# A hybrid encoder of four layers: in the latent layer, the keys' transposes stand behind the queries' projection and transposes

## The chip, the cores and the metric

The kernel runs on one core of one Trainium2 chip. The metric is device time in microseconds (us), the median of several runs; less is better. The core has a tensor engine (PE, which multiplies matrices and also transposes them, always into the accumulation memory, PSUM), a vector engine (DVE), a scalar engine (ACT), a general engine (POOL, which cannot reach PSUM here and works in the other on-chip memory, SBUF), and a queue (SP) from which nearly all transfers are issued. Each engine works through its own queue in order and waits at semaphores for the others.

## The reference

The kernel computes four residual layers, x <- x + Mixer(RMSNorm(x)), over 512 tokens of width 1024, all in 32-bit floats. Layers 0 and 3 are gated short convolutions, layer 1 is an attention over 128 keys chosen by an indexer, layer 2 is the latent attention, which the change touches:

```python
def mla_mixer(xn, positions, w_in, q_lat_norm, kv_lat_norm, w_uq, w_ukv, q_norm, k_norm, w_out):
    cq, ckv, kr, z = jnp.split(xn @ w_in, cuts, axis=-1)            # 384, 256, 32, 1024 columns
    q = (rmsnorm(cq, q_lat_norm) @ w_uq).reshape(bsz, seq, C_HEADS, C_QK)        # 16 heads of 96
    kv = (rmsnorm(ckv, kv_lat_norm) @ w_ukv).reshape(bsz, seq, C_HEADS, C_NOPE + C_V)
    k_nope, v = kv[..., :C_NOPE], kv[..., C_NOPE:]                               # 64 and 64
    k = jnp.concatenate([k_nope, jnp.broadcast_to(kr[:, :, None, :], ...)], axis=-1)
    q = rmsnorm(q, q_norm)
    k = rmsnorm(k, k_norm)
    q = jnp.concatenate([q[..., :C_NOPE], rope(q[..., C_NOPE:], positions)], axis=-1)
    k = jnp.concatenate([k[..., :C_NOPE], rope(k[..., C_NOPE:], positions)], axis=-1)
    o = dense_chunk_attention(q, k, v, C_QK ** -0.5).reshape(bsz, seq, C_WIDTH)  # chunk-causal softmax
    return (o * jax.nn.silu(z)) @ w_out
```

## The kernel before

**Tiling.** The 512 tokens are four tiles of 128 (`NT = 4`). Weights come from memory in pieces (`raw`), and ACT and POOL split each into a coarse and a fine part (`whi`, line 161, and `wlo`, line 163), in an order that is fixed by `enter` and the same for the whole program. Each projection is three matmuls on these parts (lines 287 to 289).

**The latent layer.** The 16 heads are worked in four groups of four heads. `project(g)` makes what the attention needs of a group: `keys_values(g)` first, then `queries(g)`.

- `keys_values` projects keys and values (two weight tiles by four token tiles, 512 columns, bank "pt" or "pj"). ACT copies the keys' 64 columns of each head to `kk` and the values to `v` (lines 1043, 1044), POOL squares and DVE sums them. When all four token tiles are there, POOL takes the inverse root (`small_rsqrt`) and scales `kk` (line 1057) and writes the shared rotary part beside it (line 1058). Then `finish(h)` turns the four heads.
- `queries` projects the queries (three weight tiles by four token tiles, 384 columns), ACT copies, DVE and POOL rotate (`rotate`: line 568 on POOL, 572 on DVE, 575 on POOL; the result is `qk`). Then its own `finish(h)` turns the four heads.
- A head is turned by `to_features` (line 585): four transposes of 128 tokens each into one PSUM bank `p`, then one ACT copy of 96 x 512 (line 113) to `kT` or `qT`. The bank is "tr", of which there is one; outside of an attention (`early_turns`) every second turn takes the bank "o" instead, so that two alternate.

**The attention.** It goes pair of heads by pair of heads. The scores of a pair (line 1083, tile `s`) come in chunks of 128 + 256, 384 and 512 keys and take two banks, of which there is one set; DVE adds the mask and takes the minimum (line 655), ACT takes the exponential (line 658), POOL or ACT divides by the sum (lines 673, 675), PE turns the probabilities (line 685, tile `pt`), ACT or DVE copies them (lines 690, 688), and PE multiplies with the values (line 706, tile `o`). A `Filler` steps other work in between: `project(1)`, `project(2)`, a gate projection, `project(3)`, the other gate projections (`pz`). `project(0)` and two gate projections run ahead of the attention; behind it comes the output projection (`po`).

**What sets the order.** The program is written as above, and is built with `schedule_with_timeline_sim=True`: a scheduler orders the instructions of each engine anew from the written order and what depends on what. So a small change in the written order can move instructions of every engine in this layer.

Of the kernel before, what the change touches and what calls it, by code (L numbers as in the profile page):

```python
# [71 lines left out]
def encoder(ctx: ExitStack, tc: tile.TileContext, a, out, depth=4):  # L72
# [14 lines left out]
    def tile_of(tag, name, shape=(P, S), dtype=F32):  # L87
        return sb.tile(list(shape), dtype, name=name, tag=tag, bufs=BUFS[tag])
# [4 lines left out]
    def tiny(name, n, dtype=F32, tag="tiny"):  # L93
        return sb.tile([P, n], dtype, name=name, tag=tag, bufs=24)

    def bank(name, tag):
        return ps.tile([P, S], F32, name=name, tag=tag, bufs=BANKS[tag])
# [14 lines left out]
    def copy(o, x):  # L112
        act_e.activation(o, x, AF.Copy)
# [163 lines left out]
    def small_rsqrt(v, n, scale, out=None):  # L277

        m = tiny("mean", n)
        pool.tensor_scalar(m, v, scale, EPS, op0=OP.mult, op1=OP.add)  # L280
        y = tiny("y", n) if out is None else out
        pool.tensor_tensor(out=y, in0=m, in1=minus_half[:, :n], op=OP.pow)  # L282
        return y
# [52 lines left out]
    def tokens_short(group, act, finish, tags):  # L336

        w = [x for _, u in units(group) for x in u]
        for t in range(NT):
            b = bank("pt", tags[t % len(tags)])  # L340
            for k in range(group.nk):
                products(b[:, :group.n], [y[:, t * P:(t + 1) * P] for y in act[k]], w[k], k == 0, k == group.nk - 1)
            finish(t, b)
            yield

    def by_head(x):
        return x.rearrange("p (t h) -> p t h", h=4)
# [214 lines left out]
    def rotate(o, x, C, T, bank=None):  # L562


        A, B, half = x.shape[1], x.shape[2], x.shape[4]
        pa = tile_of("rp", "ropea", (P, A, B, 2 * half))
        xf = x.rearrange("p a b i j -> p a b (i j)")
        pool.tensor_tensor(out=pa, in0=xf, in1=C.rearrange("p a i j -> p a (i j)")[:, :, None]
                                .to_broadcast([P, A, B, 2 * half]), op=OP.mult)
        pb = tile_of("rp", "ropeb", (P, A, B, 2, half))  # L570
        for i in range(2):
            dve.tensor_tensor(pb[:, :, :, i], (x if bank is None else bank)[:, :, :, 1 - i],
                                    T[:, :, None, i].to_broadcast([P, A, B, half]), op=OP.mult)
        e = dve if bank is None else pool
        e.tensor_tensor(out=o.rearrange("p a b i j -> p a b (i j)"), in0=pa,
                        in1=pb.rearrange("p a b i j -> p a b (i j)"), op=OP.add)
# [3 lines left out]
    def to_features(dst, src, n):  # L580

        turns[0] += 1
        p = bank("tr", "o" if early_turns[0] and turns[0] % 2 else "tr")
        for t in range(NT):
            pe.transpose(p[:n, t * P:(t + 1) * P], src(t), ident)  # L585
        clock[0] += 0.45
        if isinstance(dst, list):
            act_e.activation(dst[0], p, AF.Copy)
            dve.tensor_tensor(dst[1], p, dst[0].bitcast(F32), op=OP.subtract)
        else:  # L590
            copy(dst[:n], p[:n])
# [329 lines left out]
    def layer_c(last):  # L921
# [82 lines left out]
        def free(g):  # L1004

            return ["pj"] if g else ["pj", "pj", "pt", "pt"]

        def queries(g, qs, dst):
            raw = [None] * NT
            sums = tiny("hs", 16)  # L1010

            def fin(t, b):
                x = raw[t] = tile_of("qk", "qk", (P, 384))
                q = tile_of("rp", "qk2", (P, 384))
                x, b = (y.rearrange("p (h d) -> p h d", d=96) for y in (x, b[:, :384]))
                act_e.activation(x[:, :, 64:], b[:, :, 64:], AF.Copy)
                act_e.activation(q.rearrange("p (h d) -> p h d", d=96), b, AF.Square)
                dve.tensor_tensor(x[:, :, :64], b[:, :, :64], gqk[:, None].to_broadcast([P, 4, 64]), op=OP.mult)
                x5, b5 = (y[:, :, 64:].rearrange("p (a h) (i j) -> p a h i j", a=1, i=2) for y in (x, b))
                rotate(x5, x5, *(tab[:, t:t + 1] for tab in tq), b5)  # L1020
                dve.tensor_reduce(sums[:, 4 * t:4 * t + 4], q.rearrange("p (h d) -> p h d", d=96),
                                        axis=AX.X, op=OP.add)

            yield from tokens_short(a["c_uq"][g], lat["q"], fin, free(g))
            v = tiny("hv", 16)
            pool.tensor_tensor(out=by_head(v), in0=by_head(sums), in1=fq2[:, :, None].to_broadcast([P, NT, 4]),
                               op=OP.mult)
            y = small_rsqrt(v, 16, 1.0 / 96)
            pool.tensor_tensor(out=qs, in0=by_head(y), in1=fqs[:, :, None].to_broadcast([P, NT, 4]), op=OP.mult)

            def finish(h):
                to_features(dst[h], lambda t: raw[t][:, h * 96:(h + 1) * 96], 96)
            for h in range(4):
                finish(h)

        def keys_values(g, dst, vals):
            sums = tiny("hs", 16)
            ks = [tile_of("gate", "kk", (P, 4, 96)) for _ in range(NT)]

            def fin(t, b):  # L1040
                b3 = b.rearrange("p (h d) -> p h d", d=P)
                x3 = ks[t][:, :, :64]
                act_e.activation(x3, b3[:, :, :64], AF.Copy, scale=fkv[:, t:t + 1])
                act_e.activation(vals[t // 2][:, t % 2], b3[:, :, 64:], AF.Copy, scale=fkv[:, t:t + 1])
                q = tile_of("rp", "qk2", (P, 4, 64))
                pool.tensor_tensor(out=q, in0=x3, in1=x3, op=OP.mult)
                dve.tensor_reduce(sums[:, 4 * t:4 * t + 4], q, axis=AX.X, op=OP.add)

            yield from tokens_short(a["c_ukv"][g], lat["kv"], fin, free(g))
            v = tiny("hv", 16)  # L1050
            pool.tensor_tensor(out=by_head(v), in0=by_head(sums), in1=krs[:, :, None].to_broadcast([P, NT, 4]),
                               op=OP.add)
            y = small_rsqrt(v, 16, 1.0 / 96)
            for t in range(NT):
                x = ks[t]
                yt = y[:, 4 * t:4 * t + 4, None]
                pool.tensor_tensor(out=x[:, :, :64], in0=x[:, :, :64], in1=yt.to_broadcast([P, 4, 64]), op=OP.mult)
                pool.tensor_tensor(out=x[:, :, 64:], in0=krr[:, t, None].to_broadcast([P, 4, 32]),
                                   in1=yt.to_broadcast([P, 4, 32]), op=OP.mult)

            def finish(h):
                to_features(dst[h], lambda t: ks[t][:, h], 96)
            for h in range(4):
                finish(h)

        def masks(t):
            return cmask[:, S - (t + 1) * P:]
# [3 lines left out]
        def project(g):  # L1071
            s = sets[g] = dict(q=[tile_of("T", "qT") for _ in range(4)], k=[tile_of("T", "kT") for _ in range(4)],
                               v=[tile_of("v", "v", (P, 2, 4, 64)) for _ in range(2)],
                               qs=sb.tile([P, NT, 4], F32, name="qs", tag="qs", bufs=2))
            yield from keys_values(g, s["k"], s["v"])
            yield from queries(g, s["qs"], s["q"])

        def job(pair, after, fill):
            g, i = divmod(pair, 2)

            def scores(outs, t):
                for e, o in enumerate(outs):
                    pe.matmul(o, sets[g]["q"][2 * i + e][:96, t * P:(t + 1) * P],  # L1083
                              sets[g]["k"][2 * i + e][:96, :(t + 1) * P], start=True, stop=True)
                clock[0] += (t + 1) * P / 300
            return dict(scores=scores, masks=masks, after=after, fill=fill,
                        v=lambda e, t: sets[g]["v"][t // 2][:, t % 2, 2 * i + e],
                        qs=lambda e, t: sets[g]["qs"][:, t, 2 * i + e:2 * i + e + 1],
                        dst=lambda: gate[pair])

        z = a["c_z"]
        run(project(0))
        run(gate_steps(z[2:4], R, gate))
        ends = [0, 8, 16, 25, 34, 42, 50, 58, 66]
# [122 lines left out]
```

## Time and profile before

| | before |
|---|---|
| median of 3 runs | 1058.24 us (1058.1 to 1058.6) |
| the profiled execution's own time | 1058.71 us |
| its span, first to last instruction | 1056.9 us |
| granted TensorE clock, mean | 0.998 |
| PE busy in 500 to 600 us | 100.00 of 100 us |
| PE busy in 625 to 650 us (clock 0.93) | 23.32 of 25 us |
| PE busy in 650 to 675 us | 23.11 of 25 us |
| PE busy in 725 to 750 us | 23.44 of 25 us |
| PE busy in 735 to 815 us | 80.00 of 80 us |

The latent layer's work on groups of heads lies between some 608 and 815 us. A line of the timeline gives the start, the length up to the last end, the engine, the source line, the operation with what it writes and reads, the count, and in brackets how long the engine sat idle ahead of it and who ended that. PE's matmuls are pipelined: the next starts before the record of the one ahead of it ends, so that the step between two starts is shorter than a record. A line of a list of waits reads: who waited for whom, us in total, times, the longest. In a line of the windows stand the stretch and its length, then for PE, its weight loads, DVE, ACT and POOL the busy time and the number of instructions, then PE's granted clock, the transfers' share and GB/s.

### The profile page before, as it was taken

The numbers are of one execution on the slowest core, as the hardware profiler recorded it, in microseconds if no ns is written. First come the engines' busy times: TensorE is split into PE (matmuls) and PEld (weight loads), VectorE is DVE, ScalarE is ACT, GpSimd is POOL, SyncE is SP. The second block draws the span as 40 slices with busy tenths as digits, with TensorE's granted clock in tenths as the row PEclk, the third lists the DMA queues.
The fourth block names the chain that finished last, engine by engine and source line by source line (L and its number), as shares of the span: only waits on it lengthen the run. The fifth ranks groups of instructions, "written<-read, shape, count | busy, mean of one in ns | idle before, by whom it ended". The sixth has DMA issues, their size and how long they took to land.

```text
span 1056.9 us, 16253 instructions
## 1 busy us (share of the span) xinstructions
PE 1044.1 (99%) x6040; PEld 878.9 (83%) x6040; DVE 523.6 (50%) x1074; ACT 511.5 (48%) x1091; POOL 678.3 (64%) x636
## 2 busy tenths in 40 slices
PE   9999999999999999999999999999999999999998
PEld 7888888898898999898888787687777888888886
DVE  6884334335598974443435344444442664443321
ACT  6243223434444467676644446876764533333231
POOL 1546555666378799685538689788743856555552
PEclk9999999999999999999999999999999999999999
DMA  7233333224222221111213220101211333333332
GB/s 238 93 100 100 99 99 92 83 70 120 81 71 80 72 89 41 61 56 46 71 50 105 82 83 23 41 24 60 61 55 46 100 100 101 99 100 100 100 100 79
DMA packets 27295, 86.44 MB, mean 82 GB/s; under 512 B 3408, under 2 KB 4432, under 8 KB 27216
## 3 DMA queue, kind: packets, MB, share of 16 engines
q1 hardware_dynamic: 26928, 85.10, 25.9%
q8 instruction: 47, 0.77, 0.3%
q10 hardware_dynamic: 288, 0.31, 0.1%
q14 instruction: 32, 0.26, 0.1%
HBM read 83.30 MB, written 2.10 MB: 81 GB/s over the span
## 4 chain that ended last, share of the span: by engine, by line
PE 94%; DVE 2%; ACT 1%; POOL 1%; DMA 1%; issue 1%; ACTq 0%; POOLq 0%
PE pa L287 11%; PE pa L288 11%; PE pa L289 11%; PE po L287 6%; PE po L289 6%; PE po L288 6%; PE o L706 4%; PE pt L685 4%; PE s L1083 3%; PE pz L289 2%; PE pz L288 2%; PE pz L287 2%; PE s L296 2%; PE tr L585 2%; PE pq L287 2%; PE pk L288 2%
## 5 line engine op out<-in xcount | busy, mean ns | idle before, releaser
L163 POOL TENSOR_TENSOR wlo<-raw,whi 128x512 fp32r<-128x512 f32 (+4 forms) x320 | 401.4, 1262 | 281.4 <-ACT whi L161 269.4
L161 ACT ACTIVATE whi<-raw 128x512 fp32r<-128x512 f32 (+4 forms) x329 | 196.9, 603 | 328.9 <-PE pa L288 158.4
L288 PE MATMUL pa<-xl,whi 128*128 128x512 f32 x512 | 199.3, 389 | 0.0
L287 PE MATMUL pa<-xh,whi 128*128 128x512 f32 x512 | 198.2, 389 | 0.6 <-ACT xh L370 0.6
L289 PE MATMUL pa<-xh,wlo 128*128 128x512 f32 x512 | 197.6, 389 | 0.0
L287 PEld LDWEIGHTS pa<-xh,whi 128*128 128x128 f32 x512 | 96.0, 188 | 20.6 <-ACT xh L370 0.8
L288 PEld LDWEIGHTS pa<-xl,whi 128*128 128x128 f32 x512 | 96.1, 188 | 20.5 <-DVE xl L373 0.5
L289 PEld LDWEIGHTS pa<-xh,wlo 128*128 128x128 f32 x512 | 96.1, 188 | 20.0
L673 POOL TENSOR_SCALAR p<-p,rc 128x128 f32<-128x128 f32 (+1 forms) x64 | 70.2, 1103 | 45.9 <-DVE rc L668 40.6
L658 ACT ACTIVATE p<-p,mn 128x128 f32<-128x128 f32 (+3 forms) x128 | 71.0, 558 | 17.5 <-DVE mn L655 17.3
L480 DVE TENSOR_TENSOR cg<-pa,R 128x512 f32<-128x512 f32 x16 | 11.0, 690 | 118.5 <-PE pa L289 116.2
L655 DVE CUSTOM_DVE_ANT_0 p<-s,cmask,qs 128x128 f32<-128x128 f32 (+2 forms) x80 | 37.7, 506 | 33.9 <-PE s L1083 20.0
L287 PE MATMUL pz<-xh,whi 128*128 128x512 f32 x128 | 51.4, 401 | 0.0
L289 PE MATMUL pz<-xh,wlo 128*128 128x512 f32 x128 | 50.9, 398 | 0.0
L288 PE MATMUL pz<-xl,whi 128*128 128x512 f32 x128 | 50.4, 394 | 0.0
L288 PE MATMUL po<-xl,whi 128*128 128x512 f32 x128 | 50.1, 391 | 0.0
L288 PE MATMUL po<-glo,whi 128*128 128x512 f32 x128 | 49.8, 389 | 0.0
L282 POOL TENSOR_TENSOR y<-mean,minus_half 128x16 f32<-128x16 f32 (+1 forms) x18 | 49.2, 2732 | 0.8
L287 PE MATMUL po<-xh,whi 128*128 128x512 f32 x128 | 49.5, 400 | 0.0
L287 PE MATMUL po<-ghi,whi 128*128 128x512 f32 x128 | 49.5, 389 | 0.0
L690 ACT ACTIVATE p<-pt 128x384 f32<-128x384 f32 (+1 forms) x80 | 38.6, 510 | 22.0 <-PE pt L685 21.6
L685 PE MATMUL pt<-ident,p 128*128 128x128 f32 x320 | 47.9, 277 | 0.2 <-ACT p L690 0.2
(247 smaller groups left out, 2418.8 us busy)
## 6 DMA issues: line engine op xcount, KB each, us to landing
raw<-in_a_in SPq DMA_DIRECT2D x63, 512.0 KB, 3.9
raw<-in_a_out SPq DMA_DIRECT2D x16, 512.0 KB, 3.9
raw<-in_b_z SPq DMA_DIRECT2D x8, 512.0 KB, 3.5
raw<-in_b_q SPq DMA_DIRECT2D x8, 512.0 KB, 3.4
raw<-in_b_k SPq DMA_DIRECT2D x8, 512.0 KB, 3.7
raw<-in_b_v SPq DMA_DIRECT2D x8, 512.0 KB, 3.6
raw<-in_c_z SPq DMA_DIRECT2D x8, 512.0 KB, 3.6
raw<-in_b_out SPq DMA_DIRECT2D x8, 384.0 KB, 3.3
```

Of the source, the lines that this page charges most:

```text
L161: act_e.activation(hi[:, :, c], raw[:, j:j + m, c], AF.Copy)
L163: e.tensor_tensor(out=lo, in0=raw[:, j:j + m, :n - few], in1=hi[:, :, :n - few].bitcast(F32), op=OP.subtract)
L282: pool.tensor_tensor(out=y, in0=m, in1=minus_half[:, :n], op=OP.pow)
L287: nc.tensor.matmul(o, l[0], r[0], start=first, stop=False)
L288: nc.tensor.matmul(o, l[0], r[1], start=False, stop=False)
L289: nc.tensor.matmul(o, l[1], r[0], start=False, stop=last)
L655: dve.tensor_tensor_reduce(out=p[:, w], in0=banks[e][:, w], in1=j["masks"](t), scale=j["qs"](e, t), scalar=-GONE, op0=OP.add, op1=OP.min, ...
L658: act_e.activation(p[:, w], p[:, w], AF.Exp, bias=mn[e][:, i:i + 1], scale=-1.0, accum_out=sm[:, e * n + i:e * n + i + 1])
L673: pool.tensor_scalar(p[:, w], p[:, w], rc[:, i:i + 1], None, op0=OP.mult)
L685: pe.transpose(b[:, i:i + P], p[:, i:i + P], ident)
L690: act_e.activation(p[:, :n], b[:, :n], AF.Copy)
L706: pe.matmul(o[64 * e:64 * e + 64, t * P:(t + 1) * P], j["v"](e, kb), x[e][:, i:i + P], start=first, stop=t == 0)
```

## The change

In `keys_values` the loop that turned the four heads' keys goes; the function hands back the piece that turns one head, and `project` calls it for the four heads once `queries` has finished, its own turns included.

```diff
@@ keys_values
-            def finish(h):
-                to_features(dst[h], lambda t: ks[t][:, h], 96)
-            for h in range(4):
-                finish(h)
+            return lambda h: to_features(dst[h], lambda t: ks[t][:, h], 96)
...
@@ project
-            yield from keys_values(g, s["k"], s["v"])
+            turn_keys = yield from keys_values(g, s["k"], s["v"])
             yield from queries(g, s["qs"], s["q"])
+            for h in range(4):
+                turn_keys(h)
```

No instruction is added or taken away; the source lines from 1061 on move (the scores are line 1082 in the changed kernel). The transfers on SP keep their order. What the scheduler makes of it is seen at three places.

On PE, group 0, behind the last of group 1's keys' and values' projections (`pt` with 512 columns; `kk` are group 0's keys, `qk` its queries, `s` the first pair's scores, the last row begins group 1's queries' projection):

```order
 L288 MATMUL pt<-wlo,lhi 128x512
 L289 MATMUL pt<-whi,llo 128x512
-L585 MATMUL tr<-ident,kk 96x128 x16
-L585 MATMUL tr<-ident,qk 96x128 x4
+L585 MATMUL tr<-ident,qk 96x128 x12
+L585 MATMUL tr<-ident,kk 96x128 x12
+L1082 MATMUL s<-kT,qT 128x128
+L585 MATMUL tr<-ident,kk 96x128 x4
+L1082 MATMUL s<-kT,qT 128x128
+L1082 MATMUL s<-kT,qT 128x256 x2
 L287 MATMUL pt<-whi,lhi 128x384
```

Before, 16 transposes of keys and one head of queries stand here, then 18 projections, then the other three heads and the scores. After, twelve transposes of queries, the sixteen of keys and the scores stand here, and all projections behind them; four transposes of queries have gone ahead, two each among matmuls of the gate and of the projection. On POOL nothing moves up to this point: it still scales group 0's keys (lines 1057, 1058) ahead of the last two rotations (line 575).

On PE, group 2, its last three query heads before (the four key heads stand well ahead of these rows, each among other matmuls):

```order
L585 MATMUL tr<-ident,qk 96x128 x4
L1083 MATMUL s<-kT,qT 128x128
L585 MATMUL tr<-ident,qk 96x128 x4
L1083 MATMUL s<-kT,qT 128x128
L1083 MATMUL s<-kT,qT 128x256 x2
L585 MATMUL tr<-ident,qk 96x128 x4
L1083 MATMUL s<-kT,qT 128x384 x2
```

and the same heads and the keys behind them after the change (`p` are probabilities of an earlier pair, `o` its product with the values):

```order
L685 MATMUL pt<-ident,p 128x128 x6
L585 MATMUL tr<-ident,qk 96x128 x12
L585 MATMUL tr<-ident,kk 96x128 x4
L685 MATMUL pt<-ident,p 128x128 x8
L585 MATMUL tr<-ident,kk 96x128 x4
L1082 MATMUL s<-kT,qT 128x128
L706 MATMUL o<-p,v 64x128 x15
L585 MATMUL tr<-ident,kk 96x128 x4
L1082 MATMUL s<-kT,qT 128x128
L1082 MATMUL s<-kT,qT 128x256 x2
```

Four heads (twelve transposes and four) now follow each other with nothing between, and two more behind eight transposes of probabilities and behind the value matmuls. Group 1 has a like sequence, with six transposes of probabilities between some of the query heads.

On PE, group 3, after the change (`po` is the output projection; before, the key heads stand singly among matmuls of a gate, and each query head has other matmuls on both sides):

```order
L585 MATMUL tr<-ident,qk 96x128 x4
L706 MATMUL o<-p,v 64x128 x19
L585 MATMUL tr<-ident,qk 96x128 x4
L706 MATMUL o<-p,v 64x128
L585 MATMUL tr<-ident,kk 96x128 x8
L1082 MATMUL s<-kT,qT 128x128
L585 MATMUL tr<-ident,kk 96x128 x4
L1082 MATMUL s<-kT,qT 128x128
L1082 MATMUL s<-kT,qT 128x256 x2
L585 MATMUL tr<-ident,kk 96x128 x4
L287 MATMUL po<-xh,whi 128x512
```

and ACT's queue at the same place (`xh` is a gate tile's coarse part, `whi` weights of the output projection):

```order
L113 ACTIVATE qT<-tr 96x512 x3
L745 ACTIVATE xh<-gate 128x512
L113 ACTIVATE kT<-tr 96x512 x3
L658 ACTIVATE p,sum<-p,mn 128x128
L113 ACTIVATE kT<-tr 96x512
L658 ACTIVATE p,sum<-p,mn 128x256
L658 ACTIVATE p,sum<-p,mn 128x128
L658 ACTIVATE p,sum<-p,mn 128x256
L161 ACTIVATE whi<-raw 128x384
```

The last query head and the four key heads now stand together on PE, with single scores between some of them, and their copies stand together on ACT, ahead of exponentials and of a conversion of weights.

## The prediction

> **What bounds the kernel now.** I read the page's busy shares and its chain of waits first, then TensorE's list of waits in the latent layer (600 to 830 us), then its timeline there.
>
> ```profile
> span 1056.9 us, 16253 instructions
> PE 1044.1 (99%) x6040; PEld 878.9 (83%) x6040; DVE 523.6 (50%) x1074; ACT 511.5 (48%) x1091; POOL 678.3 (64%) x636
> PE 94%; DVE 2%; ACT 1%; POOL 1%; DMA 1%; issue 1%; ACTq 0%; POOLq 0%
> ```
>
> TensorE (PE) is busy for 99% and holds 94% of the chain: the kernel is as long as PE's matmuls plus PE's waits, and the change leaves all 6,040 matmuls in place. The DMA queue's order does not change at all. So the time can move by two things only: **how long PE waits, and at which clock it runs**. Nothing that ACT, POOL or DVE saves counts unless PE waits for it. In the latent layer PE waits for this:
>
> ```profile
> PE tr L585 <- ACT kT L113: 1.6, 2, 1.0
> PE s L1083 <- DVE mn L655: 1.5, 2, 1.1
> PE tr L585 <- POOL kk L1058: 1.0, 2, 0.5
> PE tr L585 <- ACT qT L113: 0.5, 1, 0.5
> PE pt L685 <- ACT p L690: 0.2, 1, 0.2
> ```
>
> That is 4.8 us shown as idle. A matmul's record lasts about 0.16 us longer than its place in the pipe, so a wait costs a little more than its idle time; below I count from start to start. The whole prize for a perfect order is some 8 us, 0.8% (4.6 in group 0, 1.8 in group 1 and 1.9 in group 2, all worked out below).
>
> **Group 0, where the keys' turns stand now.** TensorE's timeline (start, duration, operation, count, idle before):
>
> ```profile
> 638.80 0.89 PE L585 MATMUL tr<-ident,kk 128*96 128x128 f32 x4
> 640.18 0.42 PE L585 MATMUL tr<-ident,kk 128*96 128x128 f32 x2 [0.50 <-POOL kk L1058]
> 641.11 0.42 PE L585 MATMUL tr<-ident,kk 128*96 128x128 f32 x2 [0.51 <-POOL kk L1058]
> 642.11 1.57 PE L585 MATMUL tr<-ident,kk 128*96 128x128 f32 x8 [0.57 <-ACT kT L113]
> 643.50 1.09 PE L585 MATMUL tr<-ident,qk 128*96 128x128 f32 x4
> ...
> 645.03 0.52 PE L289 MATMUL pt<-whi,llo 128*128 128x384 f32 x1
> 645.35 0.52 PE L287 MATMUL pt<-whi,lhi 128*128 128x384 f32 x1
> ...
> 647.90 0.33 PE L288 MATMUL pt<-wlo,lhi 128*128 128x384 f32 x1
> 648.08 0.33 PE L289 MATMUL pt<-whi,llo 128*128 128x384 f32 x1
> 648.25 1.04 PE L585 MATMUL tr<-ident,qk 128*96 128x128 f32 x8
> 649.12 0.39 PE L1083 MATMUL s<-kT,qT 96*128 96x128 f32 x2
> ...
> 650.01 1.25 PE L1083 MATMUL s<-kT,qT 96*128 96x128 f32 x6
> 651.40 0.41 PE L287 MATMUL pt<-whi,lhi 128*128 128x384 f32 x1
> ```
>
> From 638.80 to 651.40, 12.6 us, PE does 32 transposes (eight take 649.12 - 648.25 = 0.87, so 0.11 each, 3.5 in all), 18 projections of 384 columns (0.17 each at 647.90, 3.1) and eight score passes (1.4): 8.0 us of work. The other 4.6 us are waits and a slow clock: at 645.03 a projection takes 0.32 instead of 0.17. The windows give the clock (the column behind POOL):
>
> ```profile
> 639.20:642.50 3.30, 1.66 (x10) 0.91 (x10) 0.01 (x1) 1.51 (x3) 3.25 (x8) 1.00 0.19 71
> 642.60:645.90 3.30, 3.30 (x15) 2.96 (x14) 0.55 (x2) 3.01 (x7) 3.22 (x5) 0.50 0.22 60
> 675.90:681.70 5.80, 5.80 (x40) 4.71 (x39) 2.98 (x11) 5.50 (x15) 2.17 (x3) 1.00 0.00 1
> 727.90:731.30 3.40, 2.17 (x14) 1.75 (x14) 1.44 (x9) 2.06 (x8) 3.32 (x5) 1.00 0.00 0
> ```
>
> A stretch of 3.3 us with only ten transposes is followed by one at half clock. Its price: five projections 0.15 late each (0.75), and ten or so transposes at twice 0.11, partly while PE waits anyway (0.75), 1.5 us. So group 0 holds 3.1 us of waits and 1.5 us of clock.
>
> **The same place after the change.** The keys' 16 transposes go behind the queries' 16, and the 18 projections of the next group that stood between them come after all. Four query transposes move ahead among other matmuls (4 x 0.11), so PE arrives at the other twelve at 638.80 + 0.44 = 639.24. These need the third and fourth quarter of the rotated queries, which POOL makes in the second of these rows (the first ends the scaling of the first quarter of the keys):
>
> ```profile
> 637.87 0.40 POOL L1058 TENSOR_TENSOR kk<-krr,y 128x128 f32<-128x128 f32 x1
> ...
> 641.02 0.86 POOL L575 TENSOR_TENSOR qk<-ropea,ropeb 128x128 f32<-128x128 f32 x2
> ```
>
> POOL's order is unchanged up to well behind this row: it still scales the keys first. The queries are ready at 641.45 and 641.88; the keys, ready from 638.27 on, must now wait behind them on PE. So **the wait for POOL is not removed but grows**: 2.6 us, against 1.0 idle now. Then six heads follow with nothing else between. The price of a head's turn in such a row:
>
> ```profile
> L113 ACT ACTIVATE kT<-tr x16: 573/589/604, 641.5 to 754.1; 96x512 f32<-96x512 f32 x16
> 726.81 0.60 PE L585 MATMUL tr<-ident,qk 128*96 128x128 f32 x4
> ...
> 728.09 0.64 PE L585 MATMUL tr<-ident,qk 128*96 128x128 f32 x4 [0.46 <-ACT qT L113]
> 731.35 1.56 PE L1083 MATMUL s<-kT,qT 96*128 96x384 f32 x4 [1.09 <-DVE mn L655]
> ```
>
> Four transposes end 0.60 after their start, ACT's copy takes 0.59, and with the hand-overs the bank is free again 728.09 - 726.81 = **1.28 us** after the first start. PE works 0.44 of it: a head that stands straight behind another costs 0.85 us of waiting in the attention, where all turns share the one bank "tr". Ahead of the attention two banks alternate, 0.64 per head. Walking on from 641.93 (the last query quarter): heads 2 to 7 start at 642.9, 643.5, 644.2, 644.8, 645.5 and 646.1, and the scores behind them end near 647.7. That is 8.45 us for 28 transposes and the scores (4.45): 4.0 of waits, against 3.1. **Term 0: +0.9.**
>
> For groups 1 to 3 I walked the new queues in the same way: an instruction starts when its engine is free and what it waits for has ended, with the durations of the rows of before.
>
> **Group 1.** Now:
>
> ```profile
> 657.50 1.88 PE L1083 MATMUL s<-kT,qT 96*128 96x512 f32 x4
> ...
> 661.27 1.58 PE L1083 MATMUL s<-kT,qT 96*128 96x128 f32 x8
> ...
> 664.65 1.46 PE L1083 MATMUL s<-kT,qT 96*128 96x384 f32 x4
> 667.13 0.64 PE L585 MATMUL tr<-ident,kk 128*96 128x128 f32 x4 [1.02 <-ACT kT L113]
> ...
> 670.81 1.06 PE L685 MATMUL pt<-ident,p 128*128 128x128 f32 x8 [0.18 <-ACT p L690]
> 659.81 0.73 DVE L655 CUSTOM_DVE_ANT_0 p<-s,cmask,qs 128x512 f32<-128x512 f32 x1
> 660.46 0.75 DVE L655 CUSTOM_DVE_ANT_0 p<-s,cmask,qs 128x512 f32<-128x512 f32 x1
> ```
>
> Start to start, its waits are 0.24 + 1.18 + 0.34 = 1.8. After: the second pair's scores stand straight behind the first's 512-column ones, with three transposes between. Those take 1.72 + 0.33 = 2.05, and the two score banks are free only when DVE has reduced both (1.4 more behind the scores' end; 3.77 lies between the two rows now): 1.2 to 1.7 of waiting, I take 1.3. The 512-column scores of that pair wait 0.65 for DVE in the same way, the value matmuls 0.75 and 0.3 for the copies of the probabilities, the last query head 0.65 and the first key head behind it 0.85. Sum 4.5. **Term 1: +2.7.**
>
> **Group 2.** Now 0.46 and 1.09 idle (the rows at 728.09 and 731.35), 1.9 from start to start. After, twelve query and four key transposes follow each other: three heads straight behind another, 2.55, and 0.5 at both ends. **Term 2: +1.2.**
>
> **Group 3.** Now PE never idles there, by the windows (the first number behind the length is PE's busy time):
>
> ```profile
> 735.00:815.00 80.00, 80.00 (x499) 63.20 (x500) 31.79 (x91) 51.54 (x131) 44.38 (x44) 1.00 0.19 52
> ```
>
> After, two key heads follow a query head with one matmul between (0.5 and 1.0, since ACT's queue has a conversion of the gate between two copies), a third 0.3, the output projection behind the last waits 1.3 for weights that ACT converts only behind these copies, and the next scores 0.8 for DVE. **Term 3: +3.9.**
>
> **The clock, term 4.** After the change there are three stretches of over 5 us in which PE has transposes and waits alone: group 0 from 639.24 to the first score near 645.9, group 1 (five heads among transposes of probabilities) near 5.8, group 2 near 7.7. Now there is one, 638.80 to 644.24, and it brought one half-clock stretch. At one each, that is two more at 1.5: **+3.0**. The rows speak for two readings. The 675.90 row has 40 matmuls, some of them scores, and the full clock; the 727.90 row is busy for 64% with eight transposes and scores, and the clock stays. If idle time alone decides, groups 1 and 2 are busy enough by their transposes and the term is near 0; if transposes don't count, it is larger, since the slow clock lasts until a stretch has enough matmuls. I take one each. The Trainium skill (TensorE: Matmul & The Clock Gate, "Part 4: PE-mode transpose") states that a transpose doesn't count as busy for the gate; the pair of rows at 639.20 and 642.60 agrees, but does not settle it, as PE also idled there.
>
> **Sum.** 0.9 + 2.7 + 1.2 + 3.9 + 3.0 = 11.7 us. The profiled execution took 1058.7 us (span 1056.9 and 1.8 around it), 0.5 over the runs' median of 1058.24: 1058.2 + 11.7 = **1070**.
>
> **Rivals.**
> - No further half clock: PE idles, but never so much as in the 639.20 row. The 64% busy row speaks for it. 1058.2 + 8.7 = 1067.
> - The slow clock lasts: two stretches of 3.4 us in each of the three places, six against one, 5 x 1.5 = 7.5, so 1058.2 + 8.7 + 7.5 = 1074. For it: ten transposes in 3.3 us did not keep the clock. By the skill's rule named above this one is right.
> - The waits move, but other work fills them: ACT and DVE have fewer pieces between, the copies come sooner, and 0.85 shrinks to what a head costs now. Then the order does nothing: 1058 to 1060. Against it: 1.28 us has only 0.1 of hand-over that could shrink.
> - Faster: the wait for POOL is gone, if the rotated queries are ready when PE arrives and the keys are long scaled behind them. Then group 0 loses its clock loss and most waits, 4.6 - 1.0, and the rest stays: 1054.6. It decides at 639.24: POOL would have to finish L575 2.6 us earlier, which the row at 641.02 speaks against.
>
> **How the numbers follow.** A measurement of this kernel can tell 0.2%, 2.1 us, from no change. Chances: forecast 0.45 (1068.5 to 1072), no further half clock 0.2 (1064 to 1068.5), longer half clock 0.23 (1072 to 1077), no effect 0.07, faster 0.05. The walk's waits are good to some 2 us (term 1's bounds alone are 0.5 apart, term 3 has no row of its own), so the range runs from 1063 to 1077: it holds the first three cases without their tails. Slower by over 0.2%: 0.9, within 0.2%: 0.05, faster: 0.05.
>
> **What would show it.** In the changed kernel's profile: PE "tr" waiting for POOL's qk (L575) some 2 us near 640; waits of "tr" for ACT's kT and qT of about 0.85 each, eight to ten of them, where now there are three; idle time of PE between 735 and 815 where now there is none; PEclk under 1.00 at three places instead of one. Wrong would be: heads in a row without such waits (the 1.28 us is no chain), or PE waiting as long as now and the time within 1060.

## The result, and the profile after

| | before | after |
|---|---|---|
| median | 1058.17 us (1057.85 to 1058.60) | 1069.24 us (1068.36 to 1069.99) |
| ratio, with its 95% interval | | 1.0104 [1.0091, 1.0117] |
| the profiled execution's own time | 1058.71 us | 1068.36 us |
| its span | 1056.9 us | 1066.6 us |
| granted TensorE clock, mean | 0.998 | 0.998 |

The kernel is slower by 11.1 us in the medians and by 9.7 us in the two profiled executions. The forecast was 1070. The first lines of the changed kernel's page, and TensorE's list of waits between 600 and 840 us (who waited for whom, us in total, times, the longest):

```profile
span 1066.6 us, 16250 instructions
PE 1046.0 (98%) x6040; PEld 878.5 (82%) x6040; DVE 522.8 (49%) x1074; ACT 512.9 (48%) x1091; POOL 679.4 (64%) x636
```

```profile
PE tr L585 <- ACT qT L113: 4.2, 7, 0.7
PE tr L585 <- POOL qk L575: 2.5, 2, 2.0
PE s L1082 <- DVE mn L655: 1.5, 3, 0.7
PE tr L585 <- ACT kT L113: 1.4, 2, 1.0
PE o L706 <- DVE p L688: 1.4, 3, 0.7
PE po L287 <- ACT kT L113: 1.1, 1, 1.1
PE pt L287 <- DVE ropeb L572: 0.7, 1, 0.7
...
```

PE has the same 6,040 matmuls and is busy for 1.9 us longer; its idle time in the whole list is 13.0 us (one wait of 0.2 is left out above), where it was 4.8. The 8.2 us of idle time and the 1.9 us of busy time are one thing: 20 waits stand here where 8 stood, and by the prediction's 0.16 us that a record is longer than its place in the pipe, twelve waits more are 1.9 us that count as busy. The waits for the keys on POOL are gone, and in their place stand two for POOL's rotated queries (L575), the longer one, in group 0, twice as long as both together were (2.0 against 1.0). The largest group is a turn that waits until ACT has emptied the bank of the query head before it, seven times, up to 0.7; before, it stood there once, with 0.5.

**Where the time is lost.** For the next table each kernel's PE was held against one yardstick: the mean step from one matmul's start to the next, for each form, from the trace of before with its waits left out. What a stretch takes beyond the sum of these steps is lost, by waits or by the clock. Only differences between columns count, good to some 0.3 us; the stretches are cut by time, so in a kernel that is already late their rows lie a little further on. The last four columns are the first four experiments below, in which a single group's keys are turned late.

| us lost by PE in | before | after | group 0 alone | group 1 alone | group 2 alone | group 3 alone |
|---|---|---|---|---|---|---|
| 638 to 656 (turns of group 0) | 5.1 | 5.7 | 5.7 | 4.1 | 4.2 | 5.1 |
| 656 to 712 (group 1) | 3.3 | 6.2 | 2.4 | 7.3 | 3.4 | 3.3 |
| 712 to 745 (group 2) | 3.2 | 5.4 | 3.2 | 3.7 | 7.9 | 3.1 |
| 745 to 815 (group 3) | 1.8 | 6.0 | 1.7 | 1.9 | 7.0 | 6.1 |

The change loses 0.6, 2.9, 2.2 and 4.2 us more in the four stretches, 10 us together, against 9.7 in the span.

PE's timeline after the change at three places, group 0, group 2 and group 3 (start, duration, operation, count, idle time before):

```profile
641.21 0.84 PE L585 MATMUL tr<-ident,qk 128*96 128x128 f32 x4 [2.02 <-POOL qk L575]
642.62 1.94 PE L585 MATMUL tr<-ident,qk 128*96 128x128 f32 x8 [0.57 <-ACT qT L113]
644.39 2.42 PE L585 MATMUL tr<-ident,kk 128*96 128x128 f32 x12
...
652.40 0.41 PE L287 MATMUL pt<-whi,lhi 128*128 128x384 f32 x1 [0.68 <-DVE ropeb L572]
...
720.67 0.64 PE L585 MATMUL tr<-ident,qk 128*96 128x128 f32 x4 [0.68 <-ACT qT L113]
722.00 0.64 PE L585 MATMUL tr<-ident,qk 128*96 128x128 f32 x4 [0.68 <-ACT qT L113]
723.32 0.64 PE L585 MATMUL tr<-ident,kk 128*96 128x128 f32 x4 [0.68 <-ACT qT L113]
...
726.04 1.96 PE L706 MATMUL o<-p,v 128*64 128x128 f32 x30 [0.53 <-DVE p L688]
...
782.22 0.64 PE L585 MATMUL tr<-ident,kk 128*96 128x128 f32 x4 [0.32 <-ACT qT L113]
783.82 0.64 PE L585 MATMUL tr<-ident,kk 128*96 128x128 f32 x4 [0.97 <-ACT kT L113]
...
785.14 0.64 PE L585 MATMUL tr<-ident,kk 128*96 128x128 f32 x4 [0.46 <-ACT kT L113]
...
788.44 0.50 PE L287 MATMUL po<-xh,whi 128*128 128x512 f32 x1 [1.13 <-ACT kT L113]
```

**Group 0:** PE idles 2.02 us ahead of 641.21 for POOL's last rotations. Of the keys, which stand behind them now, POOL has scaled two of the four quarters when this wait begins, the third at 639.81 and the last at 640.74. **Group 2**, from 720.67 on: three heads straight behind another, each 1.33 and 1.32 us after the one ahead, each idle for 0.68. **Group 3**, from 782.22 on: key heads behind key heads, and the first output projection 1.13 late behind the last copy. The same kernel's windows (stretch and length, then busy time and number of instructions of PE, weight loads, DVE, ACT and POOL, PE's granted clock, the transfers' share, GB/s):

```profile
639.02:642.43 3.41, 1.01 (x5) 0.34 (x4) 0.26 (x1) 1.19 (x3) 3.33 (x8) 1.00 0.14 55
642.43:645.84 3.41, 3.22 (x15) 2.67 (x16) 0.59 (x2) 2.13 (x5) 3.33 (x5) 0.50 0.22 58
717.52:720.93 3.41, 2.52 (x19) 1.78 (x18) 0.90 (x2) 2.68 (x6) 2.55 (x3) 1.00 0.11 46
720.93:724.35 3.42, 2.05 (x18) 1.55 (x17) 0.00 (x0) 1.54 (x3) 0.00 (x0) 1.00 0.00 0
735.00:815.00 80.00, 76.47 (x463) 60.12 (x462) 34.45 (x101) 53.72 (x136) 51.28 (x57) 1.00 0.18 50
```

Between 735 and 815 PE idles 3.5 us, where it idled none. And in the latent layer the clock is halved once only, in group 0, as before; in group 2, where PE has transposes and waits alone for two whole windows, it stays full.

### The profile page after: what moved, and what is told of

It is laid out like the page before. It is cut to its first block, busy times and chain, and to the rows that moved or that the text cites. A ratio compares the mean times of both kernels' runs of the same rounds, so it can differ in the third digit from the quotient of the medians.

```text
span 1066.6 us, 16250 instructions
## 1 busy us (share of the span) xinstructions
PE 1046.0 (98%) x6040; PEld 878.5 (82%) x6040; DVE 522.8 (49%) x1074; ACT 512.9 (48%) x1091; POOL 679.4 (64%) x636
## 4 chain that ended last, share of the span: by engine, by line
PE 94%; DVE 2%; ACT 2%; POOL 1%; issue 1%; DMA 1%; ACTq 0%; DVEq 0%; POOLq 0%
PE pa L287 11%; PE pa L288 11%; PE pa L289 11%; PE po L287 6%; PE po L289 5%; PE po L288 5%; PE o L706 4%; PE s L1082 3%; PE pt L685 3%; PE pz L289 2%; PE pz L287 2%; PE pz L288 2%; PE tr L585 2%; PE s L296 2%; PE pq L287 2%; PE pk L288 1%
## 5 line engine op out<-in xcount | busy, mean ns | idle before, releaser
L673 POOL TENSOR_SCALAR p<-p,rc 128x128 f32<-128x128 f32 (+1 forms) x64 | 69.9, 1098 | 70.7 <-DVE rc L668 66.5
```

The costliest lines, as they stand in the source:

```text
L673: pool.tensor_scalar(p[:, w], p[:, w], rc[:, i:i + 1], None, op0=OP.mult)
```

## The experiments

Theory A, as the expectations call it: PE's waits follow from the whole order of each queue, which the scheduler makes anew, so the price of the change isn't a sum of prices of groups. Theory B: each group's late turns have a price of their own, and these add up. Ratios are against the kernel before, with 95% intervals.

### One group alone

In the first four kernels, `e1_g0` to `e4_g3`, one group's keys are turned late and the other three groups' where they were (G is 0, 1, 2, 3):

```diff
-            for h in range(4):
-                finish(h)
+            [finish(h) for h in range(4) if g not in (G,)]
+            return finish
...
-            yield from keys_values(g, s["k"], s["v"])
-            yield from queries(g, s["qs"], s["q"])
+            turn_keys = yield from keys_values(g, s["k"], s["v"])
+            yield from queries(g, s["qs"], s["q"]); [turn_keys(h) for h in range(4) if g in (G,)]
```

> The keys' turns stand behind the queries for group 0 alone. Theory A (the time comes from PE's waits, and these depend on the whole order that the scheduler makes anew): walking this kernel's queues gives waits of +0.9 us over before, all near 640 to 650 (PE waits about 2 us for POOL's last two query rotations, then for ACT's copies). Theory B (each group has its own price and the prices add up to the 11 us): term 0 of the prediction, +0.9, and with the clock as before. Both: 1058.5 to 1060.5 us; groups 1 to 3 keep the waits of before.

> Group 1 alone. Theory A: the walk gives +5.4 us, of which some 3 lie in group 1 (scores behind scores waiting for DVE 1.4, two heads straight behind others 0.96 and 0.6) and over 1 in later groups that were not touched (value matmuls near 724, scores near 795): 1062 to 1065 us. Theory B: +2.7, 1060 to 1062 us, groups 2 and 3 as before.

> Group 2 alone. Theory A: the walk gives +7.3 us: four heads straight behind another at 0.86 each near 718 to 722, the next projection 0.84 behind the last copy, and 3.5 in group 3 and its scores, which were not touched: 1064 to 1067 us. Theory B: +1.2 to +3, 1059 to 1061.5 us. If transposes don't count as work for the clock gate, PEclk falls to half behind 718 to 726 for at least 3.4 us (+1.5); if idle time decides, it stays at 1.00.

> Group 3 alone. Theory A: the walk gives +3.0 us, with the output projection 0.9 behind ACT and score matmuls 1.8 and 0.5 behind DVE near 788 to 794, and no heads that wait 0.86: 1060.5 to 1062.5 us. Theory B: +3.9 with three heads waiting near 780, 1061.5 to 1063 us.

| late turns in | median us | ratio | us by the ratio |
|---|---|---|---|
| group 0 | 1058.47 | 1.0005 [0.9996, 1.0015] | +0.5 |
| group 1 | 1062.59 | 1.0043 [1.0028, 1.0058] | +4.6 |
| group 2 | 1068.12 | 1.0095 [1.0078, 1.0112] | +10.1 |
| group 3 | 1061.76 | 1.0038 [1.0023, 1.0053] | +4.0 |
| all four (the change) | 1069.24 | 1.0104 [1.0091, 1.0117] | +11.0 |

Group 0 alone came to the lower end of what both theories said, group 1 into theory A's range, group 3 into both ranges, and group 2 to more than both said. The four add up to 19 us and the whole change costs 11: theory B falls. The table of lost time says where. Group 1's stretch adds up (7.3 - 3.3 = 4.0 for its own edit, and 2.4 - 3.3 = -0.9 for group 0's, against 2.9 with all). Group 3's doesn't: its own edit costs 4.3 there and group 2's edit costs 5.2 there, though it leaves group 3's keys where they were; with both, 4.2. Nor is it the same loss. In the change it is mostly the key heads and the output projection that wait, as shown above. With one edit alone, the largest waits are those of the scores for DVE's minimum, 1.59 us at 794.61 in `e4_g3` and 1.53 us at 799.70 in `e3_g2`, and the window of 3.41 us behind each runs at half clock (the first two rows of the windows below), which makes its matmuls take some 1.7 us longer than by the yardstick. The edit of one group moves the work of the next, and each order has waits and slow windows of its own. That group 2 alone came to 10.1 has a second part, in group 2 itself, which its timeline and windows show:

```profile
720.44 0.64 PE L585 MATMUL tr<-ident,qk 128*96 128x128 f32 x4 [0.68 <-ACT qT L113]
...
723.09 0.64 PE L585 MATMUL tr<-ident,kk 128*96 128x128 f32 x4 [0.68 <-ACT qT L113]
724.41 0.64 PE L585 MATMUL tr<-ident,kk 128*96 128x128 f32 x4 [0.68 <-ACT kT L113]
724.89 0.39 PE L1083 MATMUL s<-kT,qT 96*128 96x128 f32 x2
725.73 1.09 PE L585 MATMUL tr<-ident,kk 128*96 128x128 f32 x4 [0.46 <-ACT kT L113]
...
799.70 2.01 PE L1083 MATMUL s<-kT,qT 96*128 96x384 f32 x4 [1.53 <-DVE mn L655]
```

```profile
795.80:799.21 3.41, 3.41 (x12) 2.40 (x11) 2.16 (x7) 2.67 (x8) 1.52 (x3) 0.50 0.00 0
800.67:804.08 3.41, 3.41 (x14) 2.45 (x13) 1.81 (x6) 2.22 (x6) 1.50 (x2) 0.50 0.01 2
...
722.16:725.57 3.41, 1.75 (x13) 1.06 (x10) 0.00 (x0) 1.67 (x3) 0.00 (x0) 1.00 0.00 0
725.57:728.98 3.41, 3.25 (x12) 2.72 (x13) 0.00 (x0) 0.70 (x2) 0.00 (x0) 0.50 0.00 0
```

The first row is `e4_g3`'s, the others are `e3_g2`'s. Five heads stand in a row here, without the eight transposes of probabilities that the change has between them. From 722.16 to 725.57 eight transposes and two scores start, and the clock is halved behind them (four transposes take 1.09 at 725.73, not 0.64). That is the loss that the prediction feared in three places; it comes in the experiments, and not in the change.

### POOL's wait in group 0

`c1_dve_keys0` leaves the written order as it was and scales group 0's keys on DVE; `c5_rot_dve` is the change with the latent layer's last rotation (L575) on DVE, so that the rotated queries no longer stand behind the keys on POOL:

```diff
# c1_dve_keys0, against before (lines 1057 and 1058)
-                pool.tensor_tensor(
+                (dve if g in (0,) else pool).tensor_tensor(
# c5_rot_dve, the change and in rotate (line 574)
-        e = dve if bank is None else pool
+        e = dve if bank is None or half == 16 else pool
```

> The kernel before, with group 0's keys scaled on DVE instead of POOL (8 instructions). Theory A (group 0's loss before is its wait for POOL, 1.0 us idle, and the half clock that follows): the keys are ready about 2 us earlier, PE's wait for POOL near 640 goes, and with less idle time the clock stays at 1.00 there: -1.6 us of waits by the walk and up to -1.5 us of clock, 1055 to 1056.5 us. Theory B (a run of transposes alone brings the half clock, whether PE idles or not): PEclk still falls to 0.5 behind 639 to 644, 1056.5 to 1057 us.

> The change, with the sum at the end of the latent layer's rotations (line 575, queries and shared key) on DVE instead of POOL. Theory A: the 2.0 us that PE waits for POOL near 640 go, since the last two rotations no longer stand behind the key scaling; the heads still stand in rows, so waits of 0.7 to 0.9 for ACT's copies stay, near 720 for four heads: the walk gives +6.5 us over before, 1062.5 to 1065 us, with the clock at 1.00 near 642. Theory B (the time lies in the rows of heads alone, POOL does not matter): as the change, 1068 to 1070 us.

`c1_dve_keys0` took 1056.30 us, ratio 0.9980 [0.9971, 0.9989]; `c5_rot_dve` 1064.45 us, 1.0053 [1.0036, 1.0070], both as theory A said. Group 0 with the late keys and without POOL's wait (PE's timeline of `c5_rot_dve`, then one of its windows in group 2):

```profile
636.86 1.03 PE L585 MATMUL tr<-ident,qk 128*96 128x128 f32 x8
...
640.49 1.03 PE L585 MATMUL tr<-ident,kk 128*96 128x128 f32 x8
642.10 0.64 PE L585 MATMUL tr<-ident,kk 128*96 128x128 f32 x4 [0.57 <-ACT kT L113]
```

```profile
718.62:722.03 3.41, 1.89 (x13) 1.13 (x11) 0.00 (x0) 1.30 (x3) 0.00 (x0) 1.00 0.00 0
```

The 2.02 us have gone, and in this execution the half clock with them: the stretch loses 2.5 us against 5.7 after the change and 5.1 before. So the wait ahead of 641.21 hangs on POOL's order, as its row says, though the scheduler made another order of PE's queue too: projections stand between the queries' and the keys' turns now. The edit moves the rotations of all four groups. The other three stretches still lose 4.2, 5.7 and 3.6 us, where the change loses 6.2, 5.4 and 6.0 and before 3.3, 3.2 and 1.8, and the kernel stays slower than before: what the change costs lies mostly in the attention, not where its wait is longest. The profiled execution is the fastest of this kernel's (1061.19 us at clock 1.000; the others 1063.87 to 1065.13 at 0.998 to 0.999), so these losses are on the low side.

### The bank that all turns share

`e9_onebank` takes from the latent layer's turns ahead of the attention their second bank; `e5_banks` gives those in the attention a second one, "pj". Both are the change, with line 583:

```diff
-        p = bank("tr", "o" if early_turns[0] and turns[0] % 2 else "tr")
# e9_onebank
+        p = bank("tr", "o" if early_turns[0] and n != 96 and turns[0] % 2 else "tr")
# e5_banks
+        p = bank("tr", ("o" if early_turns[0] else "pj" if n == 96 else "tr") if turns[0] % 2 else "tr")
```

> The change, with the one bank tr for all turns of heads in the latent layer, group 0 too. Theory A: a head straight behind another costs 0.85 us of waiting with one bank and 0.2 with two, so group 0's six heads in a row wait 0.85 each near 642 to 648, at least +2.5 us over the change; the scheduler also makes the later order anew, the walk gives +7 us over the change in all: 1073 to 1079 us. Theory B (the bank is no bound, ACT's copies are): no change, 1068 to 1071 us.

> The change, with every second turn of a head in the attention in one of the two banks pj. Theory B (a price per head times the number of heads in rows): with two banks the price falls from 0.85 to 0.2, some nine heads gain 0.65 each: 1062 to 1064 us. Theory A (the whole order decides): the waits of the turns fall in the same way, but the scheduler makes another order, in which PE waits for POOL's and DVE's work on the probabilities instead (2 to 3 us at single places near 710 and 757): 1068 to 1074 us.

`e9_onebank` took 1079.35 us (1078.16 to 1080.49), 1.0196 [1.0179, 1.0213], 0.35 us above theory A's range. Its group 0 (timeline, then a window):

```profile
643.01 1.09 PE L585 MATMUL tr<-ident,qk 128*96 128x128 f32 x4 [0.68 <-ACT qT L113]
644.78 1.09 PE L585 MATMUL tr<-ident,qk 128*96 128x128 f32 x4 [0.68 <-ACT qT L113]
```

```profile
641.20:658.20 17.00, 12.72 (x44) 9.09 (x45) 3.05 (x12) 6.95 (x16) 8.50 (x11) 0.50 0.04 12
```

With one bank the heads of group 0 queue up as those of the attention do, here 1.77 us apart since the clock is half, and it stays half for 17 us: heads in a row with their waits are too little work to bring it back. This stretch loses 12.6 us instead of 5.7.

`e5_banks` was to take 1062 to 1064 us by theory B and 1068 to 1074 by theory A. It took 1076.05 us (1073.42 to 1078.44), 1.0168 [1.0148, 1.0187]: theory B had the sign wrong, and theory A had the waits that would come, but too short. Its waits in the latent layer:

```profile
PE pt L685 <- POOL p L673: 8.6, 4, 3.8
PE s L1083 <- DVE mn L655: 4.6, 5, 1.3
...
PE tr L585 <- ACT qT L113: 0.9, 2, 0.6
...
PE tr L585 <- ACT kT L113: 0.5, 2, 0.2
```

The turns' waits for ACT fell from 5.6 us to 1.4, so it is the bank that they waited for. But the scheduler made another order of it, in which the transposes of the probabilities come up to 3.8 us too early for POOL's division (L673), 8.6 us in four waits, where the change has none. The clock is at half for 17 us more than in the change, too (from 666.99, 718.19 and 765.97 on, behind waits for DVE or POOL), which by the yardstick costs some 7 us. So this kernel shows what the turns waited for, and not what the change would cost with two banks in its own order.

### The order as written, and a spread

`f1_written_before` and `f2_written_all` are before and the change with the instructions in the written order, without the scheduler. `e6_spread` is the change with a step of the `Filler` behind each turned head, so that other work can stand between two heads:

```diff
# f1_written_before, f2_written_all
-    schedule_with_timeline_sim=True
+    schedule_with_timeline_sim=False
# e6_spread, against the change, in queries
             for h in range(4):
-                finish(h)
+                to_features(dst[h], lambda t: raw[t][:, h * 96:(h + 1) * 96], 96)
+                yield
# and in project
-            for h in range(4):
-                turn_keys(h)
+            yield from (turn_keys(h) for h in range(4))
```

> The kernel before, built without the scheduler, each engine in the written order. Much slower than before, since nothing fills PE's waits: 1130 to 1170 us by a walk of the queues. It is the base for the next run.

> The change, built without the scheduler. Theory A (the 11 us come from the order that the scheduler makes of the change, not from the later turns of the keys themselves): in the written order the change moves little or gains, since the keys' scaling on POOL has the queries' projection as cover: 0 to 4 us below the run before this one. Theory B (turning the keys behind the queries is itself what costs): about 10 us above it.

> The change, with the fill of the attention allowed to go on to other work between any two of the eight turns (a yield behind each head). Theory A: the scheduler makes nearly the same queues from it, the walk gives +9.7 us over before, and heads still wait 0.85 in rows: 1067 to 1070 us. Theory B (the four turns stand in rows because project hands them out in one piece): the heads spread among other matmuls and the time falls to 1058 to 1062 us.

The written order of before took 1195.15 us (1193.72 to 1196.44), 1.1293 [1.1277, 1.1308], that of the change 1189.22 us (1184.49 to 1189.64), 1.1227 [1.1209, 1.1245]. The first expectation was too low, the scheduler being worth 137 us; in the second, theory A had the sign, and 5.9 us lie beyond its range: in the written order the later turns *gain*. The three largest of PE's waits over the whole span, of `f1_written_before` and then of `f2_written_all`:

```profile
PE tr L585 <- POOL qk L868: 28.3, 7, 7.5
PE tr L585 <- POOL qk L575: 23.9, 13, 3.1
PE tr L585 <- POOL kk L1058: 23.2, 14, 5.5
```

```profile
PE tr L585 <- POOL qk L575: 28.4, 13, 5.1
PE tr L585 <- POOL qk L868: 28.3, 7, 7.5
PE pt L287 <- ACT qk L1017: 12.5, 2, 6.2
```

In the written order PE waits 23.2 us for the scaled keys. The late turns remove that whole row and give back 4.5 us to the rotated queries (L575) and 12.5 to a projection behind ACT's copies (L1017): 6.2 are left. The scheduler already removes nearly all of it in the order of before (1.0 us is left), so after it there is nothing to win, and only the heads in a row remain.

`e6_spread` took 1067.65 us, 1.0087 [1.0074, 1.0101], inside theory A's range. The steps part few of the heads: the scheduler still places them in rows, and PE's waits for the copies of query heads are 3.2 us in five, for those of key heads 2.3 in four, 5.5 together where the change has 5.6.

### A version faster than both

Where POOL is what the keys wait for, and DVE is busy for half of the span, the scaling itself can move. `d5_dve_keys02` is the kernel before, with `(dve if g in (0, 2) else pool)` in the lines where `c1_dve_keys0` has `(0,)`.

> The kernel before, with the keys of groups 0 and 2 scaled on DVE instead of POOL. As c1_dve_keys0 (1056.3 us), and in group 2 the order that follows drops a part of PE's 1.9 us of waits near 728 to 731: the walk gives -3.2 us of waits against before, 1.5 below c1_dve_keys0: 1054 to 1056 us, both kernels beaten. If POOL's work on the keys of group 2 is no bound, 1056 to 1057 us.

It took 1054.66 us (1054.54 to 1055.28), 0.9966 [0.9954, 0.9978], as expected. Its waits in the latent layer:

```profile
PE s L1083 <- DVE mn L655: 3.0, 4, 1.1
PE tr L585 <- DVE kk L1058: 0.8, 1, 0.8
PE tr L585 <- ACT qT L113: 0.5, 1, 0.5
PE tr L585 <- ACT kT L113: 0.4, 1, 0.4
...
```

The idle time is 5.0 us in all, not less than the 4.8 of before. The gain is elsewhere: in group 0 six projections stand between the first key head and the first transposes of the second, where before PE went from wait to wait, and the clock stays full (1.000 in the profiled execution). Against the yardstick the four stretches lose 3.2, 2.0, 2.6 and 1.4 us, where before has 5.1, 3.3, 3.2 and 1.8.

## Why the prediction was right, and where it was wrong

- **What bounds it: right.** PE keeps its 6,040 matmuls, and the 9.7 us of the span are PE's waits in the four stretches.
- **Term 0, +0.9: measured +0.6.** The wait for POOL was put at 2.6 from start to start; its row shows 2.02 idle, 2.2 with the place in the pipe. With the last rotation off POOL it goes (`c5_rot_dve`). The keys were taken as "ready from 638.27 on", which holds for their first quarter alone. A wait of 0.68 for DVE's rotation (L572), at 652.40, was not in the walk.
- **Term 1, +2.7: measured +2.9.** The waits of the walk came, the first at 0.47 idle where 1.3 was put; one of 0.51 for POOL's rotated queries, at 661.01, was not in it. The sum was right, its parts only roughly.
- **Term 2, +1.2: measured +2.2, a size.** The three heads straight behind another cost 0.68 idle, 0.85 from start to start, each, as worked out; the cycle is 1.32 to 1.33 us, not 1.28. The walk put 0.5 for both ends together; the value matmuls behind the fourth head alone wait 0.53 for DVE's copy of the probabilities, 0.7 from start to start.
- **Term 3, +3.9: measured +4.2.** Walked 0.5, 1.0, 0.3 and 1.3 for the key heads and the output projection, and 0.8 for the next scores; the rows show 0.32, 0.97, 0.46 and 1.13 idle, and 0.66 for the scores at 802.76.
- **Term 4, the clock, +3.0: wrong.** In the profiled execution it is 0: one half-clock stretch in the latent layer before, one after, in the same place, where the prediction named three as a sign. The step that failed is "stretches of over 5 us in which PE has transposes and waits alone" bringing a half clock each. Group 2's rows from 717.52 to 724.35 are such a stretch, and the clock stayed at 1.00. What counted in its place is how much PE did within one window of 3.41 us: it was busy for 74% and 60% of group 2's two windows, and for 30% of the one in group 0 (1.01 of 3.41 us) that half clock followed. The rival without a further half clock (1067) had the mechanism right; its waits were 1 us short, 8.7 against 9.7.
- **The sum.** The waits came 1 us dearer and the clock 3 us cheaper, which leaves 1068; the profiled execution took 1068.36. The median of 1069.24 lies 0.9 above that. The other runs of the change took 1068.75 to 1069.99 us at mean granted clocks of 0.998 and 0.997. A half-clock stretch more in some of them would fit, but they have no trace: that this makes up the rest of the 11.1 us is argued, not shown. That the forecast of 1070 lies within 1 us of the median is in part luck: two errors of opposite sign, 1 and 3 us, and that rest.
- **The rival "no effect" fell** on the cycle: heads in a row with one bank are a chain of 1.3 us, at half clock 1.77, and with a second bank most of the wait goes (`e5_banks`). **The rival "faster" fell** where it was said to: POOL ended 2 us after PE's arrival. Where that is mended (`c5_rot_dve`), group 0 does gain 2.6 us against before, and the other groups still take more than that.

**Open.** Why the scheduler sets heads in a row, when the written order gives it other work to set between them, isn't known. Whether the losses of the change go when other work stands between its heads, in an order fixed by hand, was not tried.

## What to carry to other kernels

Where a scheduler makes the order, an edit of the written order need not have a price of its own: read the new queue of the engine that bounds the kernel, and walk it with durations from the trace; single parts tried alone added up to 19 us here, and the whole cost 11. Turns through one bank cost their round trip (here 1.3 us, for 0.44 of work) as soon as nothing stands between them, so work that now stands scattered among other matmuls may be worth leaving scattered. When a consumer waits for a busy engine, moving the producer's work to an engine that is half idle was worth 0.3%; moving the consumer behind another consumer of the same engine only chose which of the two waits.

## What the runs showed of the hardware

**The clock asks how much PE did in one window of 3.41 us, and transposes count.** Each half-clock stretch in the traces quoted here lasts one such window or several, on a grid that is fixed within an execution. A window with transposes and waits alone was followed by half clock with 4 of them (after, 639.02), with 10 (before, near 639.20) and with 8 and two scores (`e3_g2`, 722.16). It was not with 12 (`c5_rot_dve`, 718.62; the 13th record is the end of a projection), nor with the 14 that start in the second of the change's windows of group 2 (720.93). At 0.11 us each, ten are 32% of the window and twelve 39%: the limit lies between. It isn't one limit for all matmuls: in `e4_g3` a window from 792.38 with six score passes, 43% by the yardstick of the table, was followed by half clock too. Nor is it one limit by PE's busy share: that window was busy for 54% (1.83 of 3.42 us), and one of `f1_written_before`, from 796.88 with nine projections, for 46% and kept the clock. What each kind of matmul counts wasn't tried.

The Trainium skill (TensorE: Matmul & The Clock Gate, "Part 1: The HAM clock gate") states a free-running window of 3413 ns, and the traces agree. Its "Part 4: PE-mode transpose", which says that a transpose doesn't count as busy in the same way, they contradict for the fp32 transposes of this kernel: by it the windows at 717.52 and 720.93 of the changed kernel would have been followed by half clock.

**The same queue can lose the clock or keep it.** In `e2_g1` group 0's queue on PE is that of before, with the same three idle times:

```profile
640.48 0.42 PE L585 MATMUL tr<-ident,kk 128*96 128x128 f32 x2 [0.50 <-POOL kk L1058]
641.40 0.42 PE L585 MATMUL tr<-ident,kk 128*96 128x128 f32 x2 [0.51 <-POOL kk L1058]
642.40 1.13 PE L585 MATMUL tr<-ident,kk 128*96 128x128 f32 x8 [0.57 <-ACT kT L113]
```

The eight transposes take 1.13 us here, not 1.57, and no half clock comes in the whole execution (1.000); the stretch loses 4.1 us instead of 5.1. A grid that lies elsewhere in each execution would do that, by splitting the wait between two windows. So a difference of 1 us between two runs of this kernel says nothing on its order.
